# Hybrid attention and MLP block on one core: the engines' order from the output projection's second half to the end of the up part, written by hand

## The chip, the cores and the metric

The kernel runs on one core of one Trainium2 chip. The metric is the device time of one execution in microseconds. The profile is of one execution of the program on the same chip; times inside it count from the span's start.

## The reference

One layer on a residual stream x of 1024 tokens by 1024 channels, all in float32. Two token mixers run in parallel (NSA attention and retention), a gated sum of them goes through W_out, and an MLP with a squared ReLU follows:

```python
x = x + mix @ w_out[layer]                     # 1024 x 1024
h = rmsnorm(x, norm_mlp[layer])
x = x + jnp.square(jax.nn.relu(h @ w_up[layer])) @ w_down[layer]   # 1024x4096, 4096x1024
return rmsnorm(x, norm_final)
```

Only these four lines bear on the change.

## The kernel before

Every matmul operand is split into a high and a low half of a rounded float type (`wh`, `wl` for a weight, `bh`, `bl` for an activation), and a product is three matmuls: high by high, high by low, low by high (L154). A high half is a copy on ACT into that type, a low half a subtraction on DVE of the high half from its source (L1025, L1026 for weights). PE executes in the order in which the program is written (`manual_schedule` for PE, L116); on the other engines a scheduler sets the order here. `later(d, fn)` puts a function off by d ticks, and a tick comes after every second k of a projection (L141 to L150), so that transposes stand between matmuls of the next tile.

**Output projection.** It runs in two column halves, c = 0 and 1, over eight tiles of 128 tokens in the order 0, 1, 4, 2, 5, 3, 6, 7. A tile of a half is 24 matmuls of 128x512. DVE adds x (L1161), SP stores the half to `x1_scr` (L1162). In half 1 both column halves are loaded into `x1t` (L1154, L1156), ACT squares with a sum (L194), POOL makes rstd (L188, L189), DVE applies norm and gain (L198, `norm_b`).

**Forms.** The MLP's up product is done by a seven-product (Strassen) scheme over halves of tokens, channels and hidden units. Tiles 0 to 3 are the first half of the tokens, 4 to 7 the second. `first_half` transposes a normed tile by four transposes per half into PSUM (`tp`), splits it into `bh`/`bl`, and keeps a copy `raw_t`. `second_half` joins tile j with the kept tile j-4 into the forms 2, 3, 4 (`t2h`/`t2l`, `t3h`/`t3l`, `t4h`/`t4l`) and form 1 (`bh`/`bl`), by subtractions on DVE from `tp` in PSUM (L1129 to L1132) and one on POOL (L1135, named `raw_t`), each with a split (L1109, L1110).

**Up part.** 16 blocks p of hidden units; a block has seven products of 12 matmuls. `up_raw` (L1066) loads the first half of a block's weights and splits it, `up_weights` (L1183 to L1189) the second half, and makes the weights' sums: three on POOL, one on DVE (L1188). `up_rest` runs the products in the order 2, (12,) 3, 1, 22, 4 and adds the results up out of PSUM (L1202 to L1217) with a squared ReLU (`relu2`, L1084). Then POOL forms four sums of hidden units (L1220 to L1223), and SP stores seven of them to `u_scr` (L1225).

**Down part.** Seven products of eight groups; a group needs one load of `u_scr` (L1229) and one of w_down (L1266, `y<-w_down`), each split, for 24 matmuls.

What sets the order around the change: PE's program order; one DMA queue on SP, first in first out; rings of slots for `wh`/`wl`, which a split waits for; the scheduler's choice on DVE, ACT, POOL and SP.

Of the kernel before, what the change touches and what calls it, by code (L numbers as in the profile page):

```python
# [112 lines left out]
def hybrid_block(ctx: ExitStack, tc: tile.TileContext, a: dict, out: bass.AP):  # L113
# [930 lines left out]

    with ExitStack() as e5:
        formp = e5.enter_context(tc.tile_pool(name="formp", bufs=1, side="right", reuse_waits="tile"))
        tf_ = {i: [formp.tile([P, 4, 512], F32R, name=f"t{i}{x}") for x in "hl"] for i in (2, 3, 4)}
        psW = e5.enter_context(tc.tile_pool(name="psW", bufs=6, space=PSUM, reuse_waits="tile"))
# [15 lines left out]
        def up_raw(p):  # L1064
            ra = wraw.tile([P, 1024], F32, name="raw", tag="raw")
            nc.sync.dma_start(ra, a["w_up"][:, 2 * p].rearrange("p a b -> p (a b)"))  # L1066
            sa = split_t1024(ra)
            return ra, {11: half(sa, 0), 12: half(sa, 1)}
# [16 lines left out]

        def up_first(X, ticks=False):
            p1 = headp.tile([P, 512], F32, name="p1")
            A.activation(p1, prod(X[11], 11, ticks), AF.Copy)
            return {"p1": p1}

        def up_c11(X, s, ticks=False):
            ps = prod(X[12], 21, ticks)
            s["u11"] = headp.tile([P, 512], F32, name="u11")
            V.tensor_add(s["u11"], ps, s["p1"])
            relu2(s["u11"], s["u11"])

        with ExitStack() as e6:
# [4 lines left out]
            def put_t(h, q):  # L1102
                tp = psW.tile([P, 4, P], F32, name="tp", bufs=2)
                for k in range(4):
                    T.transpose(tp[:, k], h[:, (4 * q + k) * P:(4 * q + k + 1) * P], ident)
                return tp

            def split_ps(src, H, L, eng=None):
                A.activation(H, src, AF.Copy)  # L1109
                (eng or V).tensor_tensor(L, src, H, op=OP.subtract)  # L1110

            raw_t = {}

            def first_half(h, j, q):
                tp = put_t(h, q)
                ks = slice(4 * q, 4 * q + 4)
                split_ps(tp, bh[:, ks, cols(j)], bl[:, ks, cols(j)])
                raw_t[j, q] = frm.tile([P, 4, P], F32, name=f"raw_t{q}", bufs=2)
                A.activation(raw_t[j, q], tp, AF.Copy)

            def second_half(h, j):
                i = cols(j - 4)
                js = cols(j)
                y11, y21 = raw_t[j - 4, 0], raw_t[j - 4, 1]
# [9 lines left out]
                split_ps(tp, bh[:, 4:, js], bl[:, 4:, js])  # L1134
                G.tensor_tensor(y21, y21, f2, op=OP.subtract)  # L1135
                split_ps(y12, tf_[3][0][:, :, i], tf_[3][1][:, :, i])
                split_ps(y11, bh[:, :4, js], bl[:, :4, js], G)
                split_ps(y21, tf_[4][0][:, :, i], tf_[4][1][:, :, i])

            def norm_out(j, x1t, h2, r):  # L1140
                norm_b(x1t, r, gain2, h2)
                if j < 4:
                    later(T_LAG, lambda: first_half(h2, j, 0))
                    later(T_LAG + 1, lambda: first_half(h2, j, 1))
                else:
                    later(T_LAG, lambda: second_half(h2, j))

            W = out_w(0)
            prev = None
            for c in range(2):  # L1150
                cs = slice(c * 512, (c + 1) * 512)
                for n, j in enumerate((0, 1, 4, 2, 5, 3, 6, 7)):
                    x1t = tmp.tile([P, D], F32, name="x1t")
                    nc.sync.dma_start(x1t[:, cs], a["x"][j * P:(j + 1) * P, cs])  # L1154
                    if c:
                        nc.sync.dma_start(x1t[:, :512], x1_scr[j, :, :512])  # L1156
                    ps = psW.tile([P, 512], F32, name="mmu", tag="mm")
                    dense_tok(ps, j, W)
                    if c == 0 and n == NT - 1:
                        W = out_w(1)  # L1160
                    V.tensor_add(x1t[:, cs], ps, x1t[:, cs])  # L1161
                    nc.sync.dma_start(x1_scr[j, :, cs], x1t[:, cs])  # L1162
                    if c == 0:
                        continue
                    if prev is not None:
                        norm_out(*prev)
                    h2 = tmp.tile([P, D], F32, name="h2")
                    prev = (j, x1t, h2, norm_a(x1t, h2, tmp))
            norm_out(*prev)
            raws = [up_raw(0), up_raw(1)]  # L1170
            heads = [up_first(raws[p][1], True) for p in range(2)]
            for p in range(2):
                up_c11(raws[p][1], heads[p], True)
            while due:
                tick()

        wmore = e5.enter_context(tc.tile_pool(name="wmore", bufs=1, reuse_waits="tile"))
        sfp = e5.enter_context(tc.tile_pool(name="sfp", bufs=1, reuse_waits="tile"))
        evp = e5.enter_context(tc.tile_pool(name="evp", bufs=1, reuse_waits="tile"))

        def up_weights(p, ra, X):
            rb = wraw.tile([P, 1024], F32, name="raw", tag="raw")
            nc.sync.dma_start(rb, a["w_up"][:, 2 * p + 1].rearrange("p a b -> p (a b)"))  # L1183
            F = sfp.tile([P, 3, 512], F32, name="sf")
            x11, x12, x21, x22 = ra[:, :512], ra[:, 512:], rb[:, :512], rb[:, 512:]
            G.tensor_tensor(F[:, 1], x11, x21, op=OP.subtract)
            G.tensor_tensor(x21, x21, x22, op=OP.add)
            V.tensor_sub(F[:, 0], x21, x11)  # L1188
            G.tensor_tensor(F[:, 2], x12, F[:, 0], op=OP.subtract)  # L1189
            sb = split_t1024(F[:, :2].rearrange("p a b -> p (a b)"))  # L1190
            sc = split_t1024(rb)
            sd = split_t1024(F[:, 2], 512)
            X.update({2: half(sb, 0), 3: half(sb, 1), 1: half(sc, 0), 22: half(sc, 1), 4: half(sd, 0)})
# [4 lines left out]
        def up_rest(p, X, s, first):  # L1198
            p1 = s["p1"]
            ps = prod(X[2], 2)  # L1200
            q, u3 = ev("q"), ev("u3")
            V.tensor_add(q, ps, p1)  # L1202
            if not first:
                up_c11(X, s)
            u11 = s["u11"]
            ps = prod(X[3], 3)
            V.tensor_add(u3, ps, q)
# [16 lines left out]
            for i, t in enumerate((u11, u21, u12, s2, s1, u22, s4)):  # L1224
                nc.sync.dma_start(u_scr[i][:, p], t)  # L1225
# [206 lines left out]
```

## Time and profile before

| what | value |
|---|---|
| median of three runs | 1613.12 us (1613.06 to 1617.92) |
| the profiled execution's own time | 1612.03 us |
| its span | 1610.2 us |
| PE busy | 1567.9 us, 97% |
| DVE busy | 1039.1 us, 65% |
| ACT busy | 734.3 us, 46% |
| POOL busy | 483.0 us, 30% |
| DMA | 193.93 MB, 120 GB/s over the span |

How to read it: the busy shares are means over the whole span, and each stage has its own limit. The output projection's second half lies between about 920 and 975 us, the up part between about 975 and 1291, the down part from there to the end. The profiled execution took 1.1 us less than the median of the runs.

### The profile page before, as it was taken

The numbers are of one execution on the slowest core, as the hardware profiler recorded it, in microseconds if no ns is written. First come the engines' busy times: TensorE is split into PE (matmuls) and PEld (weight loads), VectorE is DVE, ScalarE is ACT, GpSimd is POOL, SyncE is SP. The second block draws the span as 40 slices with busy tenths as digits, with TensorE's granted clock in tenths as the row PEclk, the third lists the DMA queues.
The fourth block names the chain that finished last, engine by engine and source line by source line (L and its number), as shares of the span: only waits on it lengthen the run. The fifth ranks groups of instructions, "written<-read, shape, count | busy, mean of one in ns | idle before, by whom it ended". The sixth has DMA issues, their size and how long they took to land.

```text
span 1610.2 us, 22745 instructions
## 1 busy us (share of the span) xinstructions
PE 1567.9 (97%) x7876; PEld 1306.5 (81%) x7876; DVE 1039.1 (65%) x2139; ACT 734.3 (46%) x1623; POOL 483.0 (30%) x545
## 2 busy tenths in 40 slices
PE   8999999999999999999999997999999999999998
PEld 5888887987888888888788875888888878888886
DVE  5665663574777777776655267776665567886554
ACT  5454454563767767666521144222222144443352
POOL 5110010001333223333000024655545315833550
PEclk8999999999999999999999999999999999999999
DMA  6202101252111111121644431444444388573373
GB/s 220 66 14 66 56 26 31 66 184 82 34 47 39 48 47 53 47 65 55 197 142 156 152 119 59 157 164 157 154 155 155 131 296 305 178 260 128 119 258 128
DMA packets 99347, 193.93 MB, mean 120 GB/s; under 512 B 26016, under 2 KB 28448, under 8 KB 99232
## 3 DMA queue, kind: packets, MB, share of 16 engines
q1 hardware_dynamic: 99232, 192.48, 36.2%
q8 instruction: 62, 1.02, 0.3%
q14 instruction: 53, 0.43, 0.1%
HBM read 142.11 MB, written 50.33 MB: 120 GB/s over the span
## 4 chain that ended last, share of the span: by engine, by line
PE 83%; DVE 4%; POOL 4%; ACT 3%; issue 2%; DMA 2%; SPq 0%; POOLq 0%; ACTq 0%; DVEq 0%
PE mm L154 23%; PE mmu L154 22%; PE mmd L154 16%; PE gps L154 8%; PE S L154 4%; PE O L154 3%; PE pt L890 2%; PE pt L889 2%; ACT pW L844 1%; DVE S L835 1%; PE pO L154 1%; DVE pl L892 1%; PE pc L154 1%; POOL ac L1330 1%; ACT pS L844 1%
## 5 line engine op out<-in xcount | busy, mean ns | idle before, releaser
L1025 ACT ACTIVATE wh<-raw 128x1024 fp32r<-128x1024 f32 x120 | 123.7, 1056 | 282.8 <-PE mmu L154 142.1
L1026 DVE TENSOR_TENSOR wl<-raw,wh 128x1024 fp32r<-128x1024 f32 x120 | 189.2, 1603 | 74.3 <-ACT wh L1025 74.0
L154 PE MATMUL mm<-wh,bh 128*128 128x512 f32 (+1 forms) x448 | 176.6, 394 | 1.8 <-ACT n L578 1.0
L154 PE MATMUL mmd<-wh 128*128 128x512 f32 x448 | 175.5, 392 | 2.4 <-ACT wh L1025 2.4
L154 PE MATMUL mmd<-wl,wh 128*128 128x512 f32 x448 | 175.6, 392 | 1.1 <-DVE wl L1026 0.9
L154 PE MATMUL mmd<-wh,wl 128*128 128x512 f32 x448 | 175.3, 391 | 0.0
L154 PE MATMUL mm<-wh,bl 128*128 128x512 f32 (+1 forms) x448 | 171.2, 382 | 3.2 <-DVE bl L208 3.2
L154 PE MATMUL mm<-wl,bh 128*128 128x512 f32 (+1 forms) x448 | 170.8, 381 | 0.1
L892 DVE TENSOR_TENSOR pl<-pt,ph 128x512 fp32r<-128x512 f32 (+1 forms) x160 | 103.8, 649 | 30.2 <-ACT ph L891 27.6
L188 POOL TENSOR_SCALAR msq<-ssq 128x1 f32<-128x1 f32 (+1 forms) x32 | 7.3, 227 | 385.4 <-ACT h L194 201.0
L891 ACT ACTIVATE ph<-pt 128x512 fp32r<-128x512 f32 (+1 forms) x160 | 90.4, 567 | 55.0 <-PE pt L890 51.0
L854 POOL TENSOR_SCALAR pS<-pS,cf 128x1024 f32<-128x1024 f32 (+7 forms) x64 | 47.8, 747 | 220.3 <-DVE cf L852 69.5
L835 DVE CUSTOM_DVE_ANT_0 S<-S,edge_m 128x512 f32<-128x512 f32 (+3 forms) x192 | 100.7, 530 | 14.9 <-PE S L154 12.9
L154 PE MATMUL gps<-bh,wh 128*128 128x512 f32 x256 | 108.0, 422 | 0.3 <-ACT gst L748 0.2
L154 PEld LDWEIGHTS mm<-wh,bl 128*128 128x128 f32 x448 | 84.7, 189 | 21.5 <-DVE bl L208 3.9
L154 PEld LDWEIGHTS mmd<-wh 128*128 128x128 f32 x448 | 84.7, 189 | 20.3 <-ACT wh L1025 2.8
L154 PE MATMUL mmu<-bh,wh 128*128 128x512 f32 x256 | 100.4, 392 | 0.7 <-ACT bh L1109 0.7
L154 PE MATMUL gps<-bh,wl 128*128 128x512 f32 x256 | 100.8, 394 | 0.0
L154 PE MATMUL gps<-bl,wh 128*128 128x512 f32 x256 | 100.8, 394 | 0.0
L154 PE MATMUL mmu<-bl,wh 128*128 128x512 f32 x256 | 100.2, 392 | 0.5 <-DVE bl L1110 0.5
L154 PEld LDWEIGHTS mmd<-wl,wh 128*128 128x128 f32 x448 | 84.8, 189 | 19.6 <-DVE wl L1026 1.9
L154 PE MATMUL mmu<-bh,wl 128*128 128x512 f32 x256 | 99.9, 390 | 0.0
(311 smaller groups left out, 4056.5 us busy)
## 6 DMA issues: line engine op xcount, KB each, us to landing
raw<-u_scr SPq DMA_DIRECT2D x56, 512.0 KB, 4.3
raw<-w_down SPq DMA_DIRECT2D x40, 512.0 KB, 5.1
raw<-w_up SPq DMA_DIRECT2D x32, 512.0 KB, 3.6
u_scr<-u SPq DMA_DIRECT2D x64, 256.0 KB, 2.0
u_scr<-s SPq DMA_DIRECT2D x48, 256.0 KB, 2.0
y<-w_down SPq DMA_DIRECT2D x16, 512.0 KB, 6.4
x<-x SPq DMA_DIRECT2D x8, 512.0 KB, 3.9
qt<-q_scr SPq DMA_DIRECT2D x32, 128.0 KB, 2.6
```

Of the source, the lines that this page charges most:

```text
L154: T.matmul(o, w, m, start=start, stop=stop)
L188: G.tensor_scalar(m[:, :w], ssq, 1.0 / n, EPS, op0=OP.mult, op1=OP.add)
L835: V.tensor_tensor_reduce(sc, sc, mk, -0.125, BIGPOS, OP.add, OP.min, mx[:, b:b + 1])
L844: A.activation(o, sc, AF.Exp, bias=mx[:, m:m + 1], scale=-1.0, accum_out=sums[:, b:b + 1])
L854: G.tensor_scalar(v, v, cf[:, b:b + 1], 1.0, op0=OP.mult, op1=OP.mult)
L889: T.transpose(tp[:, bi * 2], p0, ident)
L890: T.transpose(tp[:, bi * 2 + 1], p1, ident)
L891: A.activation(ph[:, :n], tp[:, :n], AF.Copy)
L892: V.tensor_sub(pl[:, :n], tp[:, :n], ph[:, :n])
L1025: A.activation(h[:, :n], r, AF.Copy)
L1026: V.tensor_sub(l[:, :n], r, h[:, :n])
L1330: G.tensor_tensor(t, t, x, op=OP.add)
```

## The change

From the output projection's second half to the end of the up part, DVE, ACT, POOL and SP also execute in written order. The program there is rewritten as a sequence of pieces.

- Transposes are copied by ACT from PSUM to SBUF (`put_t`, tiles `rt0`, `rt1`, `y12`, `y22`); splits and subtractions of the forms read those copies. There are three `tp` buffers in PSUM instead of two and five product buffers instead of six.
- The low halves t3l, t4l and bl of a form tile come after the next tile's x1 add (`lo`).
- The load of `x1t` is issued two tiles ahead.
- Block 0's first split and sums are put by ticks into the projection.
- All four sums of a block's weights are on POOL, in place in the raw tiles (`sums_1`, `sums_2`); the pool `sf` is gone.
- In the up part `more(p, k)` puts the next block's splits and loads before product k; block 14 loads the down part's first s and w_down tiles, block 15 splits them (`ahead`).
- Block 15's seven stores are issued from POOL's queue.

The diff, cut to its core:

```diff
-            def put_t(h, q):
-                tp = psW.tile([P, 4, P], F32, name="tp", bufs=2)
+            def put_t(h, q, r):
+                tp = psW.tile([P, 4, P], F32, name="tp", bufs=3)
                 for k in range(4):
                     T.transpose(tp[:, k], h[:, (4 * q + k) * P:(4 * q + k + 1) * P], ident)
+                A.activation(r, tp, AF.Copy)
...
+            def forms_1(n):
+                j = order[n]
+                js = cols(j)
+                if j < 4:
+                    for q in range(2):
+                        ks = slice(4 * q, 4 * q + 4)
+                        lo(hi(raw_t[j][q], bh[:, ks, js], bl[:, ks, js]))
+                    return
                 i = cols(j - 4)
...
-                y12 = frm.tile([P, 4, P], F32, name="y12")
+                (y11, y21), (y12, y22) = raw_t[j - 4], raw_t[j]
                 f2 = frm.tile([P, 4, P], F32, name="f2")
-                tp = put_t(h, 0)
-                A.activation(y12, tp, AF.Copy)
-                V.tensor_sub(y11, tp, y11)
-                tp = put_t(h, 1)
-                V.tensor_sub(f2, tp, y11)
-                V.tensor_sub(y12, tp, y12)
-                split_ps(f2, tf_[2][0][:, :, i], tf_[2][1][:, :, i])
+                V.tensor_sub(y11, y12, y11)
+                V.tensor_sub(f2, y22, y11)
+                t = hi(f2, tf_[2][0][:, :, i], tf_[2][1][:, :, i])
+                V.tensor_sub(y12, y22, y12)
+                lo(t)
                 G.tensor_tensor(y21, y21, f2, op=OP.subtract)
...
+            with tc.manual_schedule(engines=every):
+                load_x1(0)
+                load_x1(1)
+                load_a(0)
+                load_b(0)
+                load_a(1)
+                later(16, lambda: split_a(0))
+                later(21, lambda: sums_1(0))
+                later(26, lambda: sums_2(0, headp.tile([P, 512], F32, name="u11")))
+                for n, j in enumerate(order):
                     ps = psW.tile([P, 512], F32, name="mmu", tag="mm")
                     dense_tok(ps, j, W)
+                    x1_of(n, ps)
+                    if n > 1 and order[n - 2] >= 4:
+                        for t in raw_t[order[n - 2]]:
+                            lo(t)
+                    if n < NT - 1:
+                        if n:
+                            later(1, lambda n=n: put_of(n - 1))
+                            later(3, lambda n=n: forms_1(n - 1))
+                        later(2, lambda n=n: norm_of(n))
+                split_a(1)
+                split_2(0)
+                later(1, lambda: put_of(6))
+                later(2, lambda: norm_of(7))
+                later(3, lambda: forms_1(6))
+                later(4, lambda: put_of(7))
+                later(5, lambda: forms_1(7))
...
+        def sums_2(p, s2):
+            ra, rb = raws[p, "a"], raws[p, "b"]
+            s2w[p] = s2
+            G.tensor_tensor(s2, rb[:, 512:], ra[:, :512], op=OP.subtract)
+            G.tensor_tensor(ra[:, 512:], ra[:, 512:], s2, op=OP.subtract)
...
-            V.tensor_sub(F[:, 0], x21, x11)
...
+            elif p == 14 and k == 6:
+                split_34(p + 1)
+                ahead["s"] = s_load(0, 0)
+                ahead["t"] = wd(0, 0, 0, wraw, name="raw", tag="raw")
+            elif p == 15:
+                if k == 1:
+                    ahead[0, 0] = split_t1024(ahead["s"])
+                elif k == 2:
+                    ahead["s"] = s_load(0, 1)
+                elif k == 4:
+                    ahead[1, 0] = split_t1024(ahead["t"])
...
+            elif k == 3:
+                sums_2(p + 1, ev("s2w"))
+            elif k == 4:
+                split_2(p + 1)
+            elif k == (6 if p else 5):
+                split_34(p + 1)
+                load_a(p + 2)
+                load_b(p + 2)
...
-                nc.sync.dma_start(u_scr[i][:, p], t)
+                (nc.gpsimd if p == 15 else nc.sync).dma_start(u_scr[i][:, p], t)
```

How this moves instructions, at three places. The first is DVE in the second form tile (n = 4, token tile 5; `raw_t_10641` and `rt_10624` are the kept half of its partner tile, `f` is f2, `y` is y12 or y22). Before:

```order
L1161 TENSOR_TENSOR x1t<-mmu,x1t 128x512
L1129 TENSOR_TENSOR raw_t_10641<-tp,raw_t_10641 128x512
L1131 TENSOR_TENSOR f_10812<-tp,raw_t_10641 128x512
L1132 TENSOR_TENSOR y_10811<-tp,y_10811 128x512
L198 SCALAR_TENSOR_TENSOR h_10841<-x1t,rstd,gain 128x1024
L1110 TENSOR_TENSOR t2l<-f_10812,t2h 128x4x128
L1110 TENSOR_TENSOR bl<-tp,bh 128x4x128
L1110 TENSOR_TENSOR t3l<-y_10811,t3h 128x4x128
L1110 TENSOR_TENSOR t4l<-raw_t_10670,t4h 128x4x128
L1161 TENSOR_TENSOR x1t<-mmu,x1t 128x512
L1110 TENSOR_TENSOR bl<-tp,bh 128x4x128
```

And in the changed kernel:

```order
L198 SCALAR_TENSOR_TENSOR h_10795<-x1t,rstd,gain 128x1024
L1195 TENSOR_TENSOR rt_10624<-y_10809,rt_10624 128x512
L1196 TENSOR_TENSOR f_10842<-y_10810,rt_10624 128x512
L1198 TENSOR_TENSOR y_10809<-y_10810,y_10809 128x512
L1145 TENSOR_TENSOR t2l<-f_10842,t2h 128x4x128
L1162 TENSOR_TENSOR x1t<-mmu,x1t 128x512
L1145 TENSOR_TENSOR t3l<-y_10809,t3h 128x4x128
L1145 TENSOR_TENSOR t4l<-rt_10625,t4h 128x4x128
L1145 TENSOR_TENSOR bl<-y_10810,bh 128x4x128
L198 SCALAR_TENSOR_TENSOR h_10862<-x1t,rstd,gain 128x1024
L1145 TENSOR_TENSOR bl<-rt_10879,bh 128x4x128
L1145 TENSOR_TENSOR bl<-rt_10880,bh 128x4x128
```

The four low halves stood together behind the next norm; now only t2l does, and the other three stand behind the next tile's x1 add, before its norm. The sources `tp` have become `y` and `rt`.

The second is POOL from the second form tile to the end of the forms (L1186 to L1189 before, and L1086 to L1093 now, are the sums of a block's weights). Before:

```order
L1135 TENSOR_TENSOR raw_t_10670<-raw_t_10670,f_10812 128x512
L1110 TENSOR_TENSOR bl<-raw_t_10641,bh 128x4x128
L188 TENSOR_SCALAR msq<-ssq 128x1
L189 TENSOR_TENSOR rstd<-msq,nhalf 128x1
L1110 TENSOR_TENSOR bl<-raw_t_10762,bh 128x4x128
L1135 TENSOR_TENSOR raw_t_10791<-raw_t_10791,f_10947 128x512
L1186 TENSOR_TENSOR sf<-raw 128x512
L1187 TENSOR_TENSOR raw<-raw 128x512
L1189 TENSOR_TENSOR sf<-raw,sf 128x512
```

And in the changed kernel:

```order
L188 TENSOR_SCALAR msq<-ssq 128x1
L189 TENSOR_TENSOR rstd<-msq,nhalf 128x1
L1086 TENSOR_TENSOR raw<-raw 128x512
L1087 TENSOR_TENSOR raw<-raw 128x512
L188 TENSOR_SCALAR msq<-ssq 128x1
L189 TENSOR_TENSOR rstd<-msq,nhalf 128x1
L1092 TENSOR_TENSOR u_10829<-raw 128x512
L1093 TENSOR_TENSOR raw<-raw,u_10829 128x512
L1200 TENSOR_TENSOR rt_10625<-rt_10625,f_10842 128x512
L1203 TENSOR_TENSOR bl<-rt_10624,bh 128x4x128
```

The sums of block 0's weights stood behind the form tiles; now they stand between two of them, and there are four instead of three on POOL (one of them into `u`).

The third is DVE in the last up block and at the entry of the down part (the `wl` with L1026 are low halves; `y` is the w_down tile, `raw` an s tile or the last up weights). Before:

```order
L1210 TENSOR_TENSOR u_13308<-mmu,u_13263 128x512
L1211 TENSOR_TENSOR q<-mmu,q 128x512
L1084 SCALAR_TENSOR_TENSOR u_13308<-u_13308 128x512
L1214 TENSOR_TENSOR u_13309<-mmu,u_13263 128x512
L1084 SCALAR_TENSOR_TENSOR u_13309<-u_13309 128x512
L1026 TENSOR_TENSOR wl<-raw,wh 128x1024
L1217 TENSOR_TENSOR u_13310<-mmu,q 128x512
L1084 SCALAR_TENSOR_TENSOR u_13310<-u_13310 128x512
L1026 TENSOR_TENSOR wl<-y_13416,wh 128x1024
L1026 TENSOR_TENSOR wl<-y_13450,wh 128x1024
```

And in the changed kernel:

```order
L1324 TENSOR_TENSOR q<-mmu,p_13221 128x512
L1026 TENSOR_TENSOR wl<-raw,wh 128x1024
L1128 TENSOR_TENSOR u_13286<-mmu,p_13221 128x512
L1120 SCALAR_TENSOR_TENSOR u_13286<-u_13286 128x512
L1330 TENSOR_TENSOR u_13304<-mmu,q 128x512
L1334 TENSOR_TENSOR u_13319<-mmu,u_13304 128x512
L1335 TENSOR_TENSOR q<-mmu,q 128x512
L1120 SCALAR_TENSOR_TENSOR u_13319<-u_13319 128x512
L1026 TENSOR_TENSOR wl<-raw,wh 128x1024
L1340 TENSOR_TENSOR u_13340<-mmu,u_13304 128x512
L1026 TENSOR_TENSOR wl<-raw,wh 128x1024
L1120 SCALAR_TENSOR_TENSOR u_13340<-u_13340 128x512
```

Before, one low half (that of the first s tile) stood between the adds, and that of the first w_down tile (`y_13416`) behind the last relu. Now the first s tile's stands behind q's add, the first w_down tile's behind u22's relu (`u_13319`), and that of the second s tile one row further down.

## Rows read from the trace of the kernel before

**Rows 1.** The page, section 1: busy time of each engine, its share of the span and its instructions.

```profile
PE 1567.9 (97%) x7876; PEld 1306.5 (81%) x7876; DVE 1039.1 (65%) x2139; ACT 734.3 (46%) x1623; POOL 483.0 (30%) x545
```

**Rows 2.** The page, section 4: the chain of work that ended last, share of the span by engine.

```profile
PE 83%; DVE 4%; POOL 4%; ACT 3%; issue 2%; DMA 2%; SPq 0%; POOLq 0%; ACTq 0%; DVEq 0%
```

**Rows 3.** PE by stretch: start and end of the stretch, its length, PE's busy time (and matmuls), the granted TensorE clock as a share of full speed, the busy share of the DMA engines, GB/s.

```profile
959.00:966.00 7.00, 4.91 (x20) 0.76 0.33 112
...
983.00:990.00 7.00, 7.00 (x27) 0.77 0.05 6
...
995.00:1000.00 5.00, 4.42 (x12) 0.66 0.52 165
1000.00:1290.00 290.00, 290.00 (x1281) 1.00 0.45 153
1290.00:1293.00 3.00, 0.82 (x4) 1.00 0.98 322
1293.00:1300.40 7.40, 6.29 (x15) 0.54 0.51 194
```

**Rows 4.** PE's waits from 900 to 1320 us: the waiting operation, whom it waited for, us in total, times, the longest.

```profile
PE mmu L154 <- DVE wl L1026: 4.4, 1, 4.4
PE tp L1105 <- DVE bl L1110: 2.6, 1, 2.6
PE mmd L154 <- ACT wh L1025: 2.4, 1, 2.4
PE tp L1105 <- ACT raw_t L1119: 2.3, 2, 2.1
PE tp L1105 <- DVE raw_t L1129: 1.0, 1, 1.0
PE mmd L154 <- DVE wl L1026: 0.9, 1, 0.9
PE mmu L154 <- ACT bh L1109: 0.7, 1, 0.7
PE mmu L154 <- DVE bl L1110: 0.5, 1, 0.5
```

**Rows 5.** PE's timeline at the entry of the down part: start, duration, line, operation, and in brackets the idle time before it with who ended it.

```profile
1290.43 0.39 PE L154 MATMUL mmu<-bh,wl 128*128 128x512 f32 x1
1293.17 0.65 PE L154 MATMUL mmd<-wh 128*128 128x512 f32 x1 [2.35 <-ACT wh L1025]
...
1296.21 0.63 PE L154 MATMUL mmd<-wl,wh 128*128 128x512 f32 x1
1296.63 0.63 PE L154 MATMUL mmd<-wh,wl 128*128 128x512 f32 x1
```

**Rows 6.** DVE's timeline in the forms' stretch, columns as in the group before.

```profile
930.57 1.29 DVE L198 SCALAR_TENSOR_TENSOR h<-x1t,rstd,gain 128x1024 f32<-128x1024 f32 x1 [2.14 <-POOL rstd L189]
933.17 0.69 DVE L1161 TENSOR_TENSOR x1t<-mmu,x1t 128x512 f32<-128x512 f32 x1 [1.32 <-PE mmu L154]
...
939.57 0.69 DVE L1161 TENSOR_TENSOR x1t<-mmu,x1t 128x512 f32<-128x512 f32 x1
...
949.39 2.29 DVE L198 SCALAR_TENSOR_TENSOR h<-x1t,rstd,gain 128x1024 f32<-128x1024 f32 x1 [0.27 <-POOL rstd L189]
951.60 1.77 DVE L1110 TENSOR_TENSOR t2l<-f,t2h 128x512 fp32r<-128x512 f32 x1
953.30 0.68 DVE L1110 TENSOR_TENSOR bl<-tp,bh 128x512 fp32r<-128x512 f32 x1
953.90 0.68 DVE L1110 TENSOR_TENSOR t3l<-y,t3h 128x512 fp32r<-128x512 f32 x1
```

**Rows 7.** POOL's timeline in the forms' stretch.

```profile
949.32 1.28 POOL L1135 TENSOR_TENSOR raw_t<-raw_t,f 128x512 f32<-128x512 f32 x1
950.56 2.27 POOL L1110 TENSOR_TENSOR bl<-raw_t,bh 128x512 fp32r<-128x512 f32 x1
```

**Rows 8.** The queue of SP and then the timelines of ACT and DVE at the entry of the down part (SPq is the issuing of a DMA, with the time that its queue was held).

```profile
1281.42 6.28 SPq L1225 DMA_DIRECT2D u_scr<-u  x2
...
1292.06 1.06 ACT L1025 ACTIVATE wh<-y 128x1024 fp32r<-128x1024 f32 x1 [3.09 <-DMA y<-w_down]
1294.43 1.06 ACT L1025 ACTIVATE wh<-y 128x1024 fp32r<-128x1024 f32 x1 [1.31 <-DMA y<-w_down]
...
1289.53 1.22 DVE L1026 TENSOR_TENSOR wl<-raw,wh 128x1024 fp32r<-128x1024 f32 x1
```

**Rows 9.** ACT's timeline in the forms' stretch.

```profile
928.46 1.06 ACT L194 ACTIVATE h<-x1t 128x1024 f32<-128x1024 f32 x1 [4.12 <-DVE x1t L1161]
929.42 0.18 ACT L194 ACTIVATION_READ_ACCUMULATOR h<-x1t 128x1 f32 x1
...
940.00 0.60 ACT L1109 ACTIVATE bh<-tp 128x512 fp32r<-128x512 f32 x1
```

**Rows 10.** The up part's groups of instructions from 1000 to 1285 us: line, engine, operation, count, busy time, mean ns of one, idle time before them.

```profile
L1084 DVE SCALAR_TENSOR_TENSOR u<-u 128x512 f32<-128x512 f32 x59 | 44.6, 755 | 1.4
...
L1220 POOL TENSOR_TENSOR s<-u,u 128x512 f32<-128x512 f32 x15 | 32.1, 2143 | 71.1 <-DVE u L1084 71.1
```

**Rows 11.** Stores: the page's section 6 (DMA issues, count, KB each, median us from issue to landing), and the issue of x1's store on SP (duration in ns, min/median/max, first and last start).

```profile
u_scr<-u SPq DMA_DIRECT2D x64, 256.0 KB, 2.0
...
L1162 SPq DMA_DIRECT2D x_scr<-x1t x16: 319/326/327, 879.5 to 970.8; - x16
```

More of the change, by code (lines that the diff above doesn't have):

```diff
@@ L1112, in hybrid_block, with lo @@
[L1112 to L1121, printed above, removed]
+                A.activation(r, tp, AF.Copy)
+            def lo(t):
+                src, H, L = t
+                V.tensor_sub(L, src, H)
@@ new lines, in norm_of, with put_of @@
+            def norm_of(n):
+                norm_b(x1s[n], rs[n], gain2, h2s[n])
+                if n + 2 < NT:
+                    load_x1(n + 2)
+            def put_of(n):
+                j = order[n]
+                if n == NT - 1:
+                    y = tmp.tile([P, 2, 4, P], F32, name="x1t")
+                    r = [y[:, 0], y[:, 1]]
+                else:
+                    nm = ("rt0", "rt1") if j < 4 else ("y12", "y22")
+                    r = [frm.tile([P, 4, P], F32, name=v, bufs=2 if j < 4 else 1) for v in nm]
+                for q in range(2):
+                    put_t(h2s[n], q, r[q])
+                raw_t[j] = r
@@ L1168, in hybrid_block @@
[L1168 to L1178, printed above, removed]
@@ new lines, in hybrid_block @@
+                later(2, lambda: norm_of(7))
+                later(3, lambda: forms_1(6))
+                later(4, lambda: put_of(7))
+                later(5, lambda: forms_1(7))
+                heads = []
+                for p in range(2):
+                    prod_1(p, True)
+                    heads.append(prod(X[p][12], 21, True))
+                while due:
+                    tick()
+                l6, l7 = raw_t[6], raw_t[7]
+                lo(l6[0])
+                lo(l7[0])
+                split_34(0)
@@ new lines, in hybrid_block, with more @@
+        ahead = {}
+        def more(p, k):
+            if k == 0:
+                if p:
+                    split_b(p)
+            elif p == 14 and k == 6:
[9 more added lines that the diff above has]
+                    ahead[1, 0] = split_t1024(ahead["t"])
+            elif k == (1 if p > 1 else 2) and p:
+                split_a(p + 1)
+                if p == 1:
+                    sums_1(p + 1)
+            elif k == 2 and p:
+                sums_1(p + 1)
+            elif k == 3:
[6 more added lines that the diff above has]
+                load_b(p + 2)
@@ new lines, in slot @@
+        def slot(p, k):
+            more(p, k)
+            x, e = X[p], st[p]
+            if k == 0:
+                ps = prod(x[2], 2)
+                e["q"] = ev("q")
+                V.tensor_add(e["q"], ps, e["p1"])
+            elif k == 1:
+                out_11(p, prod(x[12], 21))
+            elif k == 2:
+                ps = prod(x[3], 3)
+                e["u3"] = ev("u3")
+                V.tensor_add(e["u3"], ps, e["q"])
+            elif k == 3:
+                ps = prod(x[1], 1)
+                e["u22"] = ev("u22")
+                V.tensor_add(e["u22"], ps, e["u3"])
+                V.tensor_add(e["q"], ps, e["q"])
+                relu2(e["u22"], e["u22"])
+            elif k == 4:
+                ps = prod(x[22], 4)
+                e["u21"] = ev("u21")
+                V.tensor_add(e["u21"], ps, e["u3"])
+                relu2(e["u21"], e["u21"])
+            elif k == 5:
+                ps = prod(x[4], 22)
+                e["u12"] = ev("u12")
+                V.tensor_add(e["u12"], ps, e["q"])
+                relu2(e["u12"], e["u12"])
+            else:
+                prod_1(p + 1)
@@ L1219, in up_rest, with hidden @@
+        def hidden(p):
+            e = st[p]
+            u11, u12, u21, u22 = e["u11"], e["u12"], e["u21"], e["u22"]
             s1, s2, s4 = ev("s1"), ev("s2"), ev("s4")
@@ L1260, in s_group @@
     def s_group(i, g):
[L1261 to L1267 removed]
+        if (i, g) == (0, 0):
+            return ahead[0, 0]
+        return split_t1024(s_raw1 if (i, g) == (0, 1) else s_load(i, g))
     def t_group(n, g):
```

209 lines of the change are left out of this document (102 added, 107 removed).

## The prediction, made before the changed kernel was run

> **What bounds the kernel now.** The busy shares of the page come first: PE is busy 97% of the span [rows 1], and PE holds 83% of the chain of work that ended last, DVE and POOL 4% each [rows 2]. So time is won only where PE stands still or runs slowly. The table of PE by stretch tells where [rows 3]: from 1000 to 1290 us, which is nearly the whole up part, PE is busy 290.00 of 290.00 us at full granted clock, 1281 matmuls at 0.226 us each; there is nothing to win there, only something to lose. The gaps lie before it, where the forms of the normed tiles are made (945 to 1000), and behind it, at the entry of the down part (1290 to 1300.4). The list of PE's waits gives both by cause [rows 4]: in the forms 4.4 + 2.6 + 2.3 + 1.0 + 0.7 + 0.5 = 11.5 us, all but a little behind low halves, copies and subtractions of DVE and ACT; at the entry 2.4 + 0.9.
>
> Two things add to the waits. Start to start a wait costs about 0.2 us more than its gap (1290.43 to 1293.17 is 2.74 us, the gap 2.35) [rows 5]; seven waits of the forms make 1.4. And behind each wait of 2 us and more the granted clock was at its lower level for a while: matmuls stand 0.42 us apart instead of 0.23 [rows 5], the stretches show 0.76, 0.77, 0.66 and 0.54 [rows 3]. Full clock less granted, times length: 7.0×0.24 + 7.0×0.23 + 5.0×0.34 = 5.0 us in the forms. So the forms lose 11.5 + 1.4 + 5.0 = 17.9. For the entry I count: 1290.0 to 1300.4 holds 4 + 15 matmuls, which at 0.226 take 4.3 of 10.4 us: 6.1 lost. **24.0 us** in all are there to be won.
>
> **The entry.** What holds PE there is a load queue and DVE's order. SP stands 6.28 us in two stores of `u` [rows 8]; behind them in its queue are the loads of w_down, ACT waits for them 3.09 and 1.31 us, and only then can low halves follow. The change issues the first s load and the first w_down load at block 14's end, splits both inside block 15 (slots 1 and 4) and issues block 15's seven stores from POOL's queue, so no load stands behind a store. The low halves of both tiles now stand on DVE ahead of u21's add (the third order above). Their cost in block 15 is two high halves (1.06 each) and two low halves (1.22 each [rows 8]) beside PE, where block 15 has no next block to split: nothing on the path. All 6.1 come back. What is late next: the stores. POOL's four sums now precede them: the first sum's 2.1 and three of at least 1.28 [rows 7, 10], after 1.4 of add and relu, so the first store is issued some 7.0 to 7.8 us past up's last matmul (E). The slots of the fourth group lie on memory that the stores read; the sixth store has to have landed (2.0 us [rows 11]) and a low half (1.22) to be done by E + 3×24×0.226 = E + 16.3. No row shows a DMA issued by POOL. At SP's 0.33 us each [rows 11] it is at 7.8 + 6×0.33 + 3.2 = 13.0, no wait; at a POOL instruction's 1.28 each, 18.7, a wait of 2.4, with a slow clock behind it of 1.7. I take 0.5, near the free end, since SP's row is the nearer kind of instruction; bounds 0 and 4.1. The Trainium skill ("DMA: Bandwidth & Descriptors", Latency and other measured facts) puts the first byte of a GpSimd-issued DMA at about 1 us where SP's path has 0.6; by that alone the store would still be in time, and no row here shows it.
>
> **The forms.** Before, DVE read the transposes in PSUM; now ACT copies them to SBUF and DVE subtracts SBUF from SBUF; the low halves of a form tile come one tile later (the first order above), and POOL's four sums for block 0 come between tiles (the second order above).
> The port first. A norm takes 1.28 us alone and 2.29 beside POOL's raw_t [rows 6, 7]; a low half with both inputs in SBUF 1.77 beside POOL and 0.68 alone; the one that reads `tp` in PSUM is 0.68 [rows 6]. POOL's own took 2.27 instead of 1.28 [rows 7]. So each meeting costs one side about 1.05. The Trainium skill states the rule ("SBUF — State Buffer", Who interferes with whom): a VectorE instruction with two SBUF inputs and a GpSimd one that reads SBUF exclude each other for the whole instruction, and one SBUF input does not; the trace agrees (2.29 against 1.28). It speaks against this change, which moves six operations per pair of tiles from PSUM to SBUF sources; by it the next sum has all eight POOL operations in the way, without it none.
>
> Then the sum, from x1's add of the fourth tile to the low half for the first up product, in the written order: 21 operations of 512 columns at 0.60 start to start [rows 6] = 12.6; four norms at 1.2, their 1.28 less the 0.08 by which rows overlap, = 4.8; waits for the norm's square and rstd, 2.15 where the norm follows the add at once (930.57 shows 2.14) and 0.3 where three operations lie between, 2×2.15 + 2×0.3 = 4.9: 22.3. POOL has eight 512-wide operations in it, 0 to 8.4 us on DVE; I take 7 of 8.4, as DVE is nearly always there to be met: 29.3. PE needs four tiles at 6.40 (933.17 to 939.57 [rows 6]) = 25.6. **3.7 left** (bounds 0 and 5.1).
>
> From the first product to the last tile's transposes DVE and ACT need a low half 0.6, x1's add 0.7, square and its read-out 1.25, one wh 1.06 queued on ACT, wl 1.13, wl 0.6, norm 1.28 = 6.6 [rows 6, 8, 9]; PE has 24 matmuls and one tile's transposes, 6.4: **0.2**. From there to form 2's product: transposes and hand-over 1.3 (6.40 less 24×0.226 is 0.96 for a tile's), seven ACT operations at 0.60 [rows 9] 4.2, f2 0.69, ACT 0.62, low half 0.7, one meeting with POOL 1.0 = 8.5 against again 6.4: **2.1** (bounds 1.0 and 3). Form 3: two low halves, one met by POOL, and wl 1.22, 3.4 against a product's 2.7: **0.7**. Form 1: add, relu, add and wl, 3.1 against 2.7: **0.4**. Low half of block 1's s2: eleven operations at about 0.62 and two meetings, 8.9 against 36 matmuls 8.2: **0.7**, and once more about **0.5** in block 1. Sum 8.3. One of these waits, the first, is over 2 us, and [rows 3, 4] show the clock lower behind each such wait at a price of 1.6 to 1.7; the waits that follow at once would hide part of it: 1.0 (bounds 0 and 3.4).
>
> **The steady blocks** are at zero now and are taken at zero: V's subtraction goes to POOL, so DVE loses 0.69 a block and POOL gains 1.28.
>
> **Sum.** Lost now 24.0; left 8.3 + 1.0 + 0.5 = 9.8; gain 14.2. The profiled execution took 1612.0, so 1597.8; the three runs' median is 1.1 above that execution: **1598.9 us**. A difference under 0.3% (4.8 us) could not be told from none.
>
> **Rivals.**
> A. The forms stay bound by DVE: the port and the copies take back what the order wins, only the entry gains, 6.1 − 0.5. For it: DVE is busy at every one of these waits, and the number of its operations hardly falls. Against it: [rows 4] has 4.4 us for one low half that stood behind others of no hurry. 1613.1 − 5.6 = 1607.5, 12%.
> B. The port hardly meets (POOL's operations fall into DVE's waits): left 8.3 − 3.7 − 1.0 − 1.0 = 2.6, no slow clock: gain 20.9, 1592.2, 12%.
> C. The stores become the entry's new wait, 4.1 instead of 0.5: 1602.5, 10%.
> D. Slower: the steady blocks become bound by the port that DVE and POOL share. A block has 84×0.226 = 19.0 us of PE. DVE's two-SBUF operations take four relus at 0.69, three wl at 1.22 and one at 0.69, 7.1 us; POOL's eight, up from seven, 10.2 at 1.28: 17.3 of 19.0. It decides when a POOL operation costs over (19.0 − 7.1)/8 = 1.49 on the mean; L1220 shows 2.1 with the time in which it is shut out [rows 10], relus 0.75 against 0.69. If one POOL operation per block does not fit, 1.3 us in 14 blocks: +18, 1617. Against it: 290.00 of 290.00 at seven. 5%.
> That the change does nothing is excluded by the order: the rows stand where it says.
>
> **Chances.** Forecast (1595 to 1604, all terms within their bounds but none at an end) 58%; A 12, B 12, C 10, D 5, other mishaps 3. The range leaves out D and the ends of A and B: low is B's 1592 less 1, high is A's 1607: 1591 to 1607. Faster by over 0.3% (under 1608.3): forecast, B, C and most of A, 0.87; same 0.07; slower 0.06.
>
> **What would show it.** Right: PE's waits for mmd gone or under 1 us, PE granted full clock at the entry; the largest wait of the forms before the first product, on the low half `bl<-rt`, 3 to 5 us; form 2's wait on t2l about 2; steady blocks without a wait. Wrong: a wait for wl in the fourth group of the down part (the stores), waits of more than 0.5 us in blocks 2 to 14 (D), or waits for transposes as many as now (A).

## The result and the profile of the changed kernel

The changed kernel's median is **1605.4 us** (1604.1 to 1609.3, six runs), the kernel before's on the same chips 1614.6. The ratio is 0.9945, with a 95% interval of 0.993 to 0.996: 9 us less, where 14.2 were forecast. In a second series of runs it was 1605.9 against 1613.8, ratio 0.9952 [0.9939, 0.9965].

The two profiled executions differ by only 2.7 us in span (1610.2 and 1607.5). To see where the time lies I cut each at two marks: DVE's first x1 add of half 2, and PE's first `mmd` matmul, with which the down part begins.

| kernel (profiled execution) | first x1 add at | to the first mmd | from there to the end |
|---|---|---|---|
| before | 922.5 | 370.7 | 317.0 |
| changed | 926.2 | 360.9 | 320.4 |
| changed, second profile | 924.2 | 360.5 | 319.0 |
| early stores (below) | 926.1 | 361.5 | 313.2 |
| early stores, sums at ticks 8 to 10 (below) | 923.2 | 359.1 | 313.2 |

Three things are to be seen. The first mark moves by up to 4 us between executions, though the order ahead of it is the same but for one load and split of weights that the kernel before has there; that is why the two spans differ so little. The stretch in which the forms are made, with the whole up part, is 10 us shorter, of which some 2.5 are the wait ahead of the first `mmd` [rows 4, 5]. And the down part is **longer by 2 to 3.4 us**, though the change was to shorten it: without any loss at its entry it takes 313.2. The two stretches together gained 6.4 us (8.2 by the second profile), less than the 9 of the medians; the rest is not located.

PE by stretch, profile of the changed kernel (columns as in [rows 3]):

```profile
957.00:965.00 8.00, 7.47 (x37) 1.00 0.29 99
...
971.00:974.40 3.40, 0.35 (x2) 1.00 0.21 77
974.40:980.00 5.60, 4.34 (x15) 0.70 0.13 47
...
1030.00:1280.00 250.00, 250.00 (x1104) 1.00 0.48 159
...
1280.00:1288.00 8.00, 8.00 (x37) 1.00 1.02 332
1288.00:1303.00 15.00, 15.00 (x68) 1.00 0.91 315
1303.00:1307.80 4.80, 0.81 (x4) 0.94 0.69 274
1307.80:1314.50 6.70, 6.68 (x17) 0.53 0.63 190
```

PE's waits in it, 900 to 1320 us (columns as in [rows 4]):

```profile
PE mmd L154 <- DVE wl L1026: 4.0, 1, 4.0
PE mmu L154 <- ACT bh L1148: 3.1, 1, 3.1
PE tp L1140 <- DVE h L198: 1.3, 2, 0.7
PE mmu L154 <- DVE bl L1145: 1.2, 1, 1.2
PE mmu L154 <- DVE wl L1026: 1.0, 3, 0.4
PE mmu L154 <- DVE t2l L1145: 0.6, 1, 0.6
```

The waits at 1290 us are gone: from 1288 to 1303 PE is busy 15.00 of 15.00, three groups of the down part. Then it stands 4.0 us at a low half of the fourth group, and runs at a granted clock of 0.53 until 1314.5, some 3.1 us more. In the forms five causes with eight waits are left, 7.2 us, the two large ones at the first up product. From 1030 to 1280 nothing is lost, with POOL's eighth operation in each block.

What the fourth group waited for shows in POOL's timeline behind the last relu:

```profile
1288.80 1.29 POOL L1354 TENSOR_TENSOR s<-u,u 128x512 f32<-128x512 f32 x1 [10.98 <-DVE u L1120]
1290.17 2.16 POOL L1355 TENSOR_TENSOR u<-u,u 128x512 f32<-128x512 f32 x1
1292.29 2.28 POOL L1356 TENSOR_TENSOR s<-s,u 128x512 f32<-128x512 f32 x1
1294.64 2.15 POOL L1357 TENSOR_TENSOR s<-u,s 128x512 f32<-128x512 f32 x1
1296.74 1.85 POOL L1359 DMA_DIRECT2D u_scr<-u  x3
1298.58 1.07 POOL L1359 DMA_DIRECT2D u_scr<-s  x2
1299.64 0.54 POOL L1359 DMA_DIRECT2D u_scr<-u  x1
```

and in DVE's:

```profile
1306.54 1.23 DVE L1026 TENSOR_TENSOR wl<-y,wh 128x1024 fp32r<-128x1024 f32 x1 [8.66 <-DMA u_scr<-u]
```

DVE stood 8.66 us for a store of `u` (u22's, whose tile was ready at 1283.8): by its place in the list of stores it is the sixth of seven behind four sums, issued at 1299.64, and DVE went on at 1306.54, as soon as it had landed. From 1270 to 1312 us such stores took this long from issue to landing (256 KB each, count, median us; compare the 2.0 of [rows 11]). SP's seven are those of block 14, 1271 to 1279 us; POOL's seven together range from 2.5, the first, to 6.8:

```profile
u_scr<-u SPq DMA_DIRECT2D x4, 256.0 KB, 4.7
u_scr<-u POOLq DMA_DIRECT2D x4, 256.0 KB, 4.8
u_scr<-s SPq DMA_DIRECT2D x3, 256.0 KB, 2.9
u_scr<-s POOLq DMA_DIRECT2D x3, 256.0 KB, 6.6
```

### The profile page after: what moved, and what is told of

It reads as the page before. It is cut to its first block, busy times and chain, and to the rows that moved or that the text cites. A ratio compares the mean times of both kernels' runs of the same rounds, so it can differ in the third digit from the quotient of the medians.

```text
span 1607.5 us, 22681 instructions
## 1 busy us (share of the span) xinstructions
PE 1566.1 (97%) x7876; PEld 1304.7 (81%) x7876; DVE 1058.4 (66%) x2123; ACT 733.1 (46%) x1627; POOL 538.8 (34%) x568
## 5 line engine op out<-in xcount | busy, mean ns | idle before, releaser
L1026 DVE TENSOR_TENSOR wl<-raw,wh 128x1024 fp32r<-128x1024 f32 x137 | 227.7, 1688 | 91.9 <-ACT wh L1025 91.9
L1025 ACT ACTIVATE wh<-raw 128x1024 fp32r<-128x1024 f32 x137 | 139.6, 1053 | 156.9 <-PE mmd L154 101.9
L154 PEld LDWEIGHTS mmd<-wh,wl 128*128 128x128 f32 x448 | 84.8, 189 | 17.7
```

The source lines that it names most:

```text
L154: T.matmul(o, w, m, start=start, stop=stop)
L1025: A.activation(h[:, :n], r, AF.Copy)
L1026: V.tensor_sub(l[:, :n], r, h[:, :n])
```

## The experiments

Theory after the comparison: the loss at the entry comes from block 15's stores, which stand in POOL's order behind the sums; what is left before the first product comes from the port (the meetings of DVE's and POOL's operations), above all from block 0's four sums. Each time below is the median of the timed runs. They stand in three series on three chips, with the kernel before at 1613.8, 1614.2 and 1615.7 us; each ratio is to the one of its own series.

**The changed kernel again.** No edit.

> The changed kernel once more, beside the kernel before on the same chip. Both theories expect the same of it: some 8 to 10 us less than before, a wait of about 4 us at the entry of the down part on a low half that waits for a store of u, and one of 3 to 4 us before the first up product. If its profiled execution is near 1604 us, the 3.7 us by which the first profile of it ran late before 900 us are that execution's own and not the change's.

1605.93 us, ratio 0.9952 [0.9939, 0.9965]. The same waits: 4.0 on a low half in the down part, 3.1 and 0.9 at the first product. Its profiled execution took 1605.5, not 1604, but its first mark lies 2 us earlier than in the first profile, with no edit.

**Stores as soon as a tile is ready.**

```diff
 (slot 1, 3, 4 of block 15, behind the relu of u11, u22, u21)
+                if p == 15:
+                    G.dma_start(u_scr[0][:, p], e["u11"])
...
             G.tensor_tensor(s1, u12, u22, op=OP.add)
+            if p == 15:
+                G.dma_start(u_scr[4][:, p], s1)
```

> Block 15's seven stores stay on POOL's queue, but each is issued as soon as its tile is ready: u11, u22 and u21 before the four sums, the other four each right behind its sum. Theory (the entry lost 4.0 us of waiting and some 3.3 us of slow clock because the stores of u21 and u22 stood behind four sums and the buffers of the down part's fourth group wait for them): the wait of 4.0 for wl is gone or under 0.5, the clock stays up, about 7 us less than the changed kernel. Rival (the low halves of groups 2 and 3, which took 2.3 us each beside POOL's sums, put DVE behind): the wait stays at 3 us or more, since the sums and the low halves still meet, and the time moves by under 2 us.

1601.67 us, ratio 0.9923 [0.9911, 0.9935]; in medians 4.3 us less than the changed kernel, where about 7 were expected, in the down part of the profile 5.8 to 7.2 less (the table: 313.2). No wait for `mmd` is left in the list of PE's waits; the rest of the list is as before:

```profile
PE mmu L154 <- ACT bh L1148: 3.1, 1, 3.1
PE tp L1140 <- DVE h L198: 1.9, 2, 1.1
PE mmu L154 <- DVE bl L1145: 1.2, 1, 1.2
PE mmu L154 <- DVE wl L1026: 0.8, 2, 0.4
```

The low halves still met POOL's sums, as the rival wanted (2.03 and 2.32 us), and it cost PE nothing. In POOL's timeline three stores now stand before the sums:

```profile
1279.18 0.76 POOL L1328 DMA_DIRECT2D u_scr<-u  x1 [0.85 <-DVE u L1120]
1284.63 0.55 POOL L1340 DMA_DIRECT2D u_scr<-u  x1 [4.69 <-DVE u L1120]
1288.09 0.54 POOL L1347 DMA_DIRECT2D u_scr<-u  x1 [2.90 <-DVE u L1120]
```

**Stores back on SP.** One word: `nc.gpsimd` to `nc.sync` for block 15, behind the sums.

> Of the changed kernel only the queue of block 15's seven stores is undone: SP in place of POOL, in the same place behind the four sums. Theory (it is the place behind the sums that costs, on either queue): on SP the loads of the down part's groups 2 and later stand behind the stores until about 1297, PE waits 4 to 6 us for a split of group 2 instead of one of the fourth, the time is within 3 us of the changed kernel's. Rival (POOL's way of issuing costs, and SP's does not): the wait is under 2 us and the time 4 to 6 us less.

1606.92 us, ratio 0.9963 [0.9949, 0.9976]: the time of the changed kernel within 1.5 us, as the theory said, but not in the way that it said. PE's waits from 1290 us to the end:

```profile
PE mmd L154 <- DVE wl L1026: 3.5, 2, 2.6
PE mmd L154 <- ACT wh L1025: 0.9, 2, 0.6
```

Only 0.8 and 0.3 of it are at the entry, under the 2 us that the rival gave; the other 2.6 and 0.6 come at 1396 to 1400 us, in the second product. The loads behind the stores left SP from 1295.5 on, some 10 us later than in the changed kernel. That the late wait follows from them is likely and not shown. Nor did the edit keep the place behind the sums for every store: SP does not execute the sums, and it issued u11's and u21's stores ahead of them, at 1277.25 and 1285.51 us. So this run does not tell the queue from the place; the run with early stores, on POOL's queue as in the changed kernel, does.

**Sums and first split early.**

```diff
-                later(16, lambda: split_a(0))
-                later(21, lambda: sums_1(0))
-                later(26, lambda: sums_2(0, headp.tile([P, 512], F32, name="u11")))
+                later(4, lambda: split_a(0))
+                later(6, lambda: sums_1(0))
+                later(8, lambda: sums_2(0, headp.tile([P, 512], F32, name="u11")))
```

> Only block 0's first split and four sums are moved to an earlier part of the projection (ticks 4, 6 and 8 in place of 16, 21 and 26), ahead of the first form tile. Theory (the port: the four sums each lengthened one DVE operation by about 1.05 us between the fourth tile and the first product): those norms and low halves fall from 2.31, 2.36 (two), 2.31 and 1.76 us to 1.28, 1.29 and 0.69, DVE reaches the first product's low half 4 us earlier, the waits of 3.1 and 1.2 us there and the two of 0.5 to 0.7 for transposes fall to about 1 in all, the clock stays up: 5 to 6.5 us less than the changed kernel. Rival (the chain of norm, square and rstd and the number of operations set it): under 2 us less.

1608.04 us, 2 us more than the changed kernel: a miss. DVE's low half of the split waited for ACT's high half, which waited for the load of its weights, and stood ahead of the first x1 add (DVE's timeline):

```profile
928.79 1.23 DVE L1026 TENSOR_TENSOR wl<-raw,wh 128x1024 fp32r<-128x1024 f32 x1 [9.20 <-ACT wh L1025]
929.93 0.68 DVE L1162 TENSOR_TENSOR x1t<-mmu,x1t 128x512 f32<-128x512 f32 x1
```

PE's waits up to 1000 us, the first two rows:

```profile
PE tp L1140 <- DVE h L198: 4.9, 1, 4.9
PE mmu L154 <- DVE bl L1145: 1.2, 1, 1.2
```

But the wait at the first product fell from 3.1 + 1.2 to 1.2, as the theory has it. The 4.9 us that PE stood before gave DVE time too, so this run alone does not show why; the one with ticks 8 to 10 does.

**Both edits.**

> Both edits together. Theory: they act in separate stretches, so the gains add, 12 to 13 us less than the changed kernel, some 21 less than before, near 1592. Rival: if either is not the cause, less by that part.

1602.43 us, ratio 0.9932 [0.9919, 0.9946]; the down part is 313.2 us, and the wait of 5.0 for the first norm is there again. No gain over the early stores, for the reason just seen.

**Early stores, sums in the middle.** The early stores, and the same three lines with ticks 8, 9 and 10.

> The early stores, and block 0's first split and four sums at ticks 8, 9 and 10 instead of 16, 21 and 26: behind the landing of their weights (which held DVE and x1's add in the run with ticks 4, 6 and 8) and still ahead of the first form tile. Theory (the port; the sums took 4.2 us from DVE's chain): the wait for a norm of 5 us is gone, the wait at the first product is about 1.2 us as in that run, the clock stays up: 5 to 6 us less than with the early stores alone, near 1596. Rival (moving them only moves the delay): a new wait of several us between tiles 1 and 3, and no more than 2 us gained.

**1597.37 us**, ratio 0.9897 [0.9882, 0.9912]: the version that beats both. DVE's timeline at the places at which the changed kernel showed the meetings, first the changed kernel:

```profile
956.46 2.31 DVE L198 SCALAR_TENSOR_TENSOR h<-x1t,rstd,gain 128x1024 f32<-128x1024 f32 x1 [0.44 <-POOL rstd L189]
958.69 2.36 DVE L1145 TENSOR_TENSOR bl<-rt,bh 128x512 fp32r<-128x512 f32 x2
...
963.78 2.31 DVE L198 SCALAR_TENSOR_TENSOR h<-x1t,rstd,gain 128x1024 f32<-128x1024 f32 x1 [2.13 <-POOL rstd L189]
966.01 1.76 DVE L1195 TENSOR_TENSOR rt<-y,rt 128x512 f32<-128x512 f32 x1
```

and with the sums moved:

```profile
955.91 1.28 DVE L198 SCALAR_TENSOR_TENSOR h<-x1t,rstd,gain 128x1024 f32<-128x1024 f32 x1 [0.44 <-POOL rstd L189]
957.11 1.29 DVE L1145 TENSOR_TENSOR bl<-rt,bh 128x512 fp32r<-128x512 f32 x2
...
961.13 1.28 DVE L198 SCALAR_TENSOR_TENSOR h<-x1t,rstd,gain 128x1024 f32<-128x1024 f32 x1 [2.13 <-POOL rstd L189]
962.33 0.68 DVE L1195 TENSOR_TENSOR rt<-y,rt 128x512 f32<-128x512 f32 x1
```

Four rows (one of two operations), each 1.03 to 1.08 us shorter: 4.2 us of DVE. From the fourth x1 add to the end of the first product's low half DVE took 26.7 us instead of 30.8. PE's waits at the first product fell from 4.3 to 2.1 (0.9 and 1.2); the first stretch from 361.5 to 359.1. Form 2 now waits 1.5 (t2h 0.4, t2l 1.1), which the larger wait ahead of it had hidden.

The rival, that the move only moves the delay, holds in part: where the sums now stand, the fourth x1 add comes 21.5 us behind the first, instead of 18.7 to 19.7. What is left of the 4.2 is 1.4 to 2.4 us by the table. The medians show 4.3 less than the early stores alone, on another chip; of the two profiles' difference 2.9 us lie ahead of the first mark, where nothing is changed.

**Low halves later still.** t3l and bl of a form tile one tile on, t4l as it was.

> As the run before, and the low halves t3l and bl of a form tile one tile later still, where DVE waits 2.1 us for rstd anyway. If DVE's chain with its waits for the norm is what is left before the first product, its wait of 1.2 us falls to under 0.5 and the time by 0.5 to 1.5 us; if that wait is set by the transposes and ACT's copies, nothing moves.

1597.93 us, ratio 0.9902 [0.9885, 0.9918]: no difference that these runs can tell. In the trace the waits before form 2 fell from 3.7 to 1.9 (transposes 0.5, first product 0.6 and 0.8) and the first stretch from 359.1 to 357.4 us, so the mechanism holds, by less than was expected (the wait of 1.2 fell to 0.8, not under 0.5), and its gain is below what the runs resolve.

**Low halves of tiles 0 to 3 from PSUM.** The source of `lo` and `hi` is `tp` again for j < 4.

> Of the changed kernel only one thing is undone: the splits of token tiles 0 to 3 read the transposes in PSUM again (the copies to SBUF are still made). The sums and stores stay late. Theory (a low half with both inputs in SBUF excludes POOL's reads, one with PSUM does not): the two low halves that took 2.36 us beside POOL's sum take 1.28, norms with both inputs in SBUF still take 2.3, the wait at the first product falls by about 1 us. Rival (POOL's traffic slows any DVE operation): they stay at 2.3.

1605.66 us, ratio 0.9947 [0.9933, 0.9962], the changed kernel's time. DVE's rows:

```profile
955.55 2.31 DVE L198 SCALAR_TENSOR_TENSOR h<-x1t,rstd,gain 128x1024 f32<-128x1024 f32 x1 [0.44 <-POOL rstd L189]
957.78 1.28 DVE L1146 TENSOR_TENSOR bl<-tp,bh 128x512 fp32r<-128x512 f32 x2
```

and POOL's beside them:

```profile
956.85 2.13 POOL L1087 TENSOR_TENSOR raw<-raw 128x512 f32<-128x512 f32 x1
```

The pair reading PSUM took 1.28 where the pair reading SBUF took 2.36, beside the same POOL operation; the norm, both inputs in SBUF, kept its 2.31. The waits at the first product fell by 0.6 (to 2.7 and 1.0), where about 1 was expected, those for transposes from 1.3 to 0.3; the time did not show it. That decides against a general slowing: a low half with one input in PSUM is not lengthened beside POOL, one with both in SBUF is.

**The split of the first w_down tile behind the last relu.** On the version with ticks 8 to 10, `split_t1024(ahead["t"])` is moved from slot 4 to behind slot 5.

> As the run with early stores and the sums at ticks 8 to 10, but the split of the first w_down tile, loaded ahead as there, stands in the written order behind the last relu instead of between the adds of block 15. Theory (the entry of the kernel before lost its 6.1 us half to DVE's order, since low halves stood behind the last relu, and not to the loads alone): the first group's second matmul waits for that low half, add and relu 1.4 plus 1.2 to 2.3 us, a wait of 2.5 to 3.5 us and a slow clock behind it, 4 to 6 us more than that run. Rival (only the loads behind the stores mattered): under 1 us more.

1602.11 us, ratio 0.9916 [0.9900, 0.9932], against 1598.36 of that version beside it. PE waits 2.4 us on the low half, just under what was expected, and the down part takes 317.5 instead of 313.2: 4.3 us for one split's place in the order (its high half on ACT moves with it). DVE's rows: of the two low halves behind the last relu the first, for which PE waits, took 1.22 us, as it does alone; only the second, 2.29, met POOL's sum.

```profile
1283.84 0.69 DVE L1120 SCALAR_TENSOR_TENSOR u<-u 128x512 f32<-128x512 f32 x1
1284.45 3.43 DVE L1026 TENSOR_TENSOR wl<-raw,wh 128x1024 fp32r<-128x1024 f32 x2
```

**The kernel before with early stores.** The same early stores in the kernel before, all else unchanged.

> The kernel before with one thing changed: block 15's seven stores are issued from POOL's queue as soon as their tiles are ready, all else as the scheduler orders it. Theory (the load queue and DVE's order each held the entry): the loads of w_down are issued some 6 us earlier and ACT no longer waits 3.1 us for them, but the low half still stands behind the last relu, so PE waits 2 to 3.5 us at the entry instead of 2.4 + 0.9, and the time falls by 0 to 3 us. Rival (SP's queue alone held it): the entry's 6 us are gone.

1611.98 us against 1615.71, ratio 0.9978 [0.9969, 0.9988]: 3.7 less, a little over the 3 expected at most. In the profile the two stretches (369.9 and 316.4) are 1.4 us shorter than before. The first load of w_down leaves SP 8 us ahead of u12's add, where it left 3 ahead. PE's waits at the entry:

```profile
PE mmd L154 <- DVE wl L1026: 1.2, 1, 1.2
PE mmd L154 <- ACT wh L1025: 0.9, 1, 0.9
```

and DVE's rows there, behind ACT's for the first high half of w_down:

```profile
1295.68 1.06 ACT L1025 ACTIVATE wh<-y 128x1024 fp32r<-128x1024 f32 x1 [1.66 <-PE mmu L154]
...
1296.63 0.69 DVE L1084 SCALAR_TENSOR_TENSOR u<-u 128x512 f32<-128x512 f32 x1
1297.25 3.44 DVE L1026 TENSOR_TENSOR wl<-y,wh 128x1024 fp32r<-128x1024 f32 x2
```

The load queue was a part of the old loss (3.3 us of waits became 2.1). Of the rest, 1.2 is the low half behind the last relu; the other 0.9 is that high half, for which ACT had waited 1.66 us for PE and not for a load. That third cause the prediction did not name.

**The best version again.**

> The run with early stores and the sums at ticks 8 to 10 once more, to stand beside the two others on the same chip: near 1597, some 16 to 17 us less than before.

1598.36 us, ratio 0.9893 [0.9871, 0.9915].

## Why the prediction held, and where it was off

**The time and the range.** Of the 14.2 us forecast 9.1 came. The 1605.4 lies outside the 1595 to 1604 that carried 58%, and inside 1591 to 1607 only because the range was drawn up to the time of rival A, whose mechanism did not happen: that it is in range is luck. One of the prediction's own signs of being wrong came true, a wait for wl in the fourth group of the down part.

**What held.** PE was the place to read, and the two gaps were the right ones. The steady blocks stayed at zero (250.00 of 250.00), so rival D fell. In the forms 17.9 were lost and 8.3 + 1.0 forecast to be left; by the same reckoning [rows 3, 4] the changed kernel leaves 7.2 of waits, 8 × 0.2, and 5.6 × 0.30 = 1.7 of slow clock, **10.5**. The table gives the same: 10 us less, 2.5 of it the entry's, so 7.3 to 7.7 won of 8.6 forecast. Within it the largest term was too small and the later ones too large. At the first product stand 3.1 + 1.2, two starts and the slow clock, 6.4 instead of 4.7, and 1.3 for transposes ahead of it; the later waits come to 0.6 + 1.0 instead of 4.6, form 2's to 0.6 instead of 2.1, since a wait gives DVE time.

From the fourth tile's x1 add at 945.26 to the end of the product's low half DVE took 30.8 us, 1.5 more than the 29.3 of the sum. The meetings are not what was missing. Eight DVE rows are longer there than alone, together by 7.0 us, just what was taken: four beside block 0's sums by 1.03 to 1.08, and in each of two form tiles t2l by 0.9 and t3l by 0.5 beside POOL's two operations of the tile. The rows of the first, with t4l as one that meets nothing:

```profile
951.51 1.60 DVE L1145 TENSOR_TENSOR t2l<-f,t2h 128x512 fp32r<-128x512 f32 x1
...
953.64 1.18 DVE L1145 TENSOR_TENSOR t3l<-y,t3h 128x512 fp32r<-128x512 f32 x1
954.74 0.68 DVE L1145 TENSOR_TENSOR t4l<-rt,t4h 128x512 fp32r<-128x512 f32 x1
```

What was missing is 0.3 in the waits for rstd (5.2 instead of 4.9) and 0.7 at four places where a row starts 0.78 or 0.79 behind the one before it instead of 0.60 (as at 949.33 and 950.12); the rest is smaller gaps. Rival A (the forms stay bound) is excluded, and rival B (the port hardly meets) too: all eight met.

**What was off: the term for the stores, 0.5 with bounds 0 and 4.1.** It measured 4.0 of waiting, 0.2 for the start and 3.1 of slow clock, 7.3 by PE's rows, and 5.8 to 7.2 by the table (319.0 and 320.4 against 313.2). That eats about the whole 6.1 that the entry won. Three of its factors were too small. The sums took 1.29 + 2.16 + 2.28 + 2.15 = 7.9 us instead of 6.4, as three of the four met low halves of the groups behind, where the prediction let one do so; the first store left 9.6 us behind up's last matmul (1287.1), not 7.8. A store costs POOL 0.54 (the first 0.76) instead of the 0.33 taken. And the sixth took 6.7 us to land (1299.64 to 1306.3) instead of 2.0: the DMA engines were busy 0.91 of the time from 1288 to 1303 with loads of u_scr and w_down. The price of 2.0 was a median over the whole kernel before, taken into a stretch in which it does not hold. Rival C named the mechanism with 10% and priced it at 4.1; at its measured price it gives 1598.9 − 0.5 + 7.3 = 1605.7, beside 1605.4 measured. That this is so near is in part luck too: the forms left 1.2 more than forecast, and the kernel before's median came 1.4 higher in the six runs than in the three that the sum starts from.

**The form of the error.** The prediction called SP's row "the nearer kind of instruction" and took the term near its free end. Both ends were built from quiet rows, so the upper bound did not hold. That the stores of ready tiles stood behind sums that they do not need could be read in the code; the run with early stores is that one edit, and it brings the down part to 313.2 and the time to 1601.7, inside 1595 to 1604; with the sums moved it is 1597.4.

**The port and the path of the stores.** The rule of the Trainium skill ("SBUF — State Buffer", Who interferes with whom) was borne out by the run from PSUM, 1.28 us against 2.36. Of the 1 us against 0.6 of the Trainium skill ("DMA: Bandwidth & Descriptors", Latency and other measured facts): no run here shows the first byte by itself. The store did not land in time, but by these rows the path was the smaller part of it: with the engines busy 0.44 of the time a store from POOL landed in 2.7 us (the kernel before with early stores, 1286.76), and with 0.63 SP's in 2.0 to 2.5 (the run with stores on SP, from 1290.62 on); the sixth store's 6.7 came at 0.96.

**Still open.** Why the stretch ahead of the first mark varies by 4 us between executions, and what sets the late wait at 1396 us with the stores on SP. Nor does a run take back the order of the forms' low halves, ACT's copies or the earlier loads of `x1t` each by itself: which of them won the 7.3 to 7.7 us of the forms is argued from the rows, not shown.

## What to carry to other kernels

When an in-order queue takes over stores, look at what stands ahead of each one in that order, and let the ones that are ready go first. Price a transfer by rows of the stretch in which it will run, not by the median over the kernel. And when operations move from one memory to another, write down which of their neighbours on the other engine now exclude them: here four sums at another time of the same stretch, and an order of seven stores, were together worth 8 us in the medians, nearly as much as the whole change had won (9.1).

## What the hardware showed that was not expected

A 256 KB store issued by POOL held that engine 0.54 us (the first 0.76). In the changed kernel it landed after 2.5 us (the first of the seven) to 6.8 (the last), with the DMA engines 0.89 to 0.96 busy; the median of SP's stores over the whole kernel before is 2.0. A DVE pair with one input in PSUM ran at 1.28 us beside a POOL operation that stretched the same pair with SBUF inputs to 2.36. And equal waits were not followed by an equal loss of clock. In the version with ticks 8 to 10 the granted clock was 0.79 from 984 to 990 us, behind waits of 0.4 and 1.1 us; in its repeat the same two waits were followed by 1.00. Behind the store's 4.0 us the next 6.7 us had 0.53 in the first profile of the changed kernel and 0.79 in the second, which covers the difference between the table's 320.4 and 319.0.
